# Layer 0's opening: modulation weights summed 512 wide, block 0 half by matmul, and four chunks normalised on GpSimd

## The chip, the cores and the metric

The kernel runs on one core of a Trainium2 chip. The number that counts is the device time of one execution in microseconds (us), on that core. TensorE (PE) does matmuls and transposes, VectorE (DVE), ScalarE (ACT) and GpSimd (POOL) do elementwise work, SyncE (SP) issues the DMAs.

## The reference

Two decoder layers over 512 tokens of 1024 channels, in float32. What the change touches is the beginning of layer 0: the modulation of the normalised input and the first columns of the input projection.

```python
mod = jax.nn.silu(c) @ w_ada + b_ada
shift, scale, gate = jnp.split(mod, 3, axis=-1)
h = rms_norm(x, g_norm) * (1.0 + scale[:, None, :]) + shift[:, None, :]
z = h @ w_in
```

`c` is one vector of 1024 values, `w_ada` has 3 x 1024 columns per layer. Three token mixers (forgetting attention, sparse attention with an indexer, stick-breaking attention), their merge and an output projection follow; none of that is changed.

## The kernel before

Channels lie on the 128 partitions and tokens along the free axis, so `x` is eight chunks (k = 0 to 7) of 128x512. Every float32 matmul is made of three: each operand is split into a high part (`hi`, L117, a copy on ScalarE) and a low part (`lo`, L121, a subtraction, on VectorE), and high x high, low x high and high x low are added in PSUM (`mm3`). The names `wh`/`wl`, `hH`/`hL`, `tm`/`pr` are such pairs, for weights, for the normalised and modulated input, and for two gate columns' weights.

`first_layer` is layer 0's opening, the first 77 us or so. In it the order of VectorE, ScalarE and GpSimd is the program's own, written out by hand (as PE's and SP's are throughout), so an instruction waits for the one written before it on its engine.

- The eight transposed chunks `xc` (`mix`) and the row of 1/rms values are made; `rb` is that row broadcast over the partitions, in PSUM. `norm(k)` multiplies: `xn[k] = xc[k] * rb` (`vs<-mix,pt`, L886).
- The rest goes in four blocks b = 0 to 3, of 256 channels, two chunks each. `load_ada(b)` loads the shift and the scale weights of the block (eight k chunks of 128 input channels, each 128x256 for shift, part 0, and for scale, part 1). `ada_sums(b)` makes silu(c) times weights, summed over the input channels: k = 0 to 3 are scaled in place by ScalarE (L895) and added by GpSimd (L897), k = 4 to 7 are multiplied and added by VectorE (`scalar_tensor_tensor`, L902). The two sums (`fm` for scale, `tmp` for shift) are summed over partitions by matmuls of one column against ones (`pa`), and VectorE adds the biases (`mod`, L911, L914).
- `chunks(b)` does the multiply and add of scale and shift on two chunks (VectorE, L930), then `hi` and `lo` into `hH`, `hL`.
- `unit(u, b)` is a unit of six 512-column matmuls that adds the block's two chunks into the output column u. u = 0 to 3 are single columns (weights `wt`, split for four chunks at a time by `split_single`), u = 4 and 5 the gate columns (weights from `split_gates(b)`, `tm` and `pr`).

PE's order per block is units 0, 1, 4, 5 of block b, then the `pa` matmuls of block b+1, then units 2 and 3 of block b. In block 3 the rope tables (`rope_tables`, L242 to L270) and the small projection's weights follow on VectorE and ScalarE instead of a next block's sums.

## Time and profile before

| what | value |
|---|---|
| median of 3 runs | 1300.32 us (1298.90 to 1304.62) |
| the profiled execution | 1303.22 us |
| its span in the profile | 1301.3 us |
| mean granted clock of PE | 0.983 |
| PE busy | 1237.4 us, 95% of the span |
| VectorE busy | 978.0 us, 75% |
| ScalarE busy | 728.3 us, 56% |
| GpSimd busy | 170.2 us, 13% |

The span runs from the first to the last instruction that the profile shows; the execution is 1.9 us longer. Times below are counted from the span's start. [...]

### The profile page before, as it was taken

Reading aid. Unit: us, or ns where it says so; the run is one execution under the profiler, and the core shown is the slowest. Engines: PE = TensorE matmul, PEld = TensorE weight load, DVE = VectorE, ACT = ScalarE, POOL = GpSimd, SP = SyncE. Lnnn points to the kernel's source line nnn. Section 1 sums busy time; section 2 is a strip of 40 time slices with the busy share of each in tenths; the row PEclk is TensorE's granted clock in tenths of the full one; section 3 lists DMA queues with packets and bytes.
Section 4 is the critical chain, followed back from the end, with each engine's and each line's share of the span. In section 5 each row is a group of like instructions: output and inputs, shape, how many; then the busy total and the mean of one; then the engine's idle time right before and its main releaser. Section 6 shows DMA issues by size and latency. Waiting matters only on the chain.

```text
span 1301.3 us, 19557 instructions
## 1 busy us (share of the span) xinstructions
PE 1237.4 (95%) x6970; PEld 1073.9 (83%) x6970; DVE 978.0 (75%) x2065; ACT 728.3 (56%) x1450; POOL 170.2 (13%) x367
## 2 busy tenths in 40 slices
PE   4799999999899899999999999999999999999997
PEld 4689888888778688888899988897887888888887
DVE  6768887799999768675667877788898975756553
ACT  5367766575445555554335766666544475665343
POOL 3302132222112000000000212222201100000000
PEclk7899999999999999999999999999999999999999
DMA  9543333233322333444442423223223222323331
GB/s 322 150 142 98 98 98 87 78 113 100 111 74 74 98 98 97 113 119 126 143 131 82 115 65 98 71 76 97 69 78 83 80 81 82 97 70 118 90 105 73
DMA packets 192433, 133.33 MB, mean 102 GB/s; under 512 B 9456, under 2 KB 187200, under 8 KB 192336
## 3 DMA queue, kind: packets, MB, share of 16 engines
q1 hardware_dynamic: 188720, 125.72, 33.4%
q10 hardware_dynamic: 3616, 6.37, 1.5%
q8 instruction: 55, 0.90, 0.3%
q14 instruction: 42, 0.34, 0.1%
HBM read 125.74 MB, written 6.29 MB: 101 GB/s over the span
## 4 chain that ended last, share of the span: by engine, by line
PE 63%; DVE 19%; DMA 8%; issue 4%; ACT 4%; POOL 1%; SPq 0%; DVEq 0%; POOLq 0%; ACTq 0%
PE pg L65 49%; PE pt L65 7%; DMA raw<-in_w_in_dram 5%; PE pa L65 4%; DVE wl L121 3%; PE pt L69 3%; DVE fm L595 2%; ACT wh L117 2%; DVE ada L278 2%; DVE m L541 1%; DVE score L542 1%; DVE pr L596 1%; DVE pt L121 1%; DMA y<-in_w_ada_dram 1%; DVE qst L123 1%
## 5 line engine op out<-in xcount | busy, mean ns | idle before, releaser
L65 PE MATMUL pg<-hH,wh 128*128 128x512 f32 (+1 forms) x824 | 330.1, 401 | 2.0 <-ACT hH L117 1.8
L65 PE MATMUL pg<-hH,wl 128*128 128x512 f32 (+1 forms) x824 | 322.5, 391 | 0.8 <-DVE wl L121 0.8
L65 PE MATMUL pg<-hL,wh 128*128 128x512 f32 (+1 forms) x824 | 322.1, 391 | 0.0
L121 DVE TENSOR_TENSOR wl<-raw,wh 128x1024 fp32r<-128x1024 f32 (+1 forms) x174 | 212.4, 1222 | 102.2 <-ACT wh L117 100.5
L117 ACT ACTIVATE wh<-raw 128x1024 fp32r<-128x1024 f32 (+1 forms) x174 | 183.3, 1055 | 152.2 <-PE pg L65 84.4
L65 PEld LDWEIGHTS pg<-hH,wl 128*128 128x128 f32 x824 | 156.8, 190 | 34.8 <-DVE wl L121 1.0
L65 PEld LDWEIGHTS pg<-hH,wh 128*128 128x128 f32 x824 | 157.3, 191 | 26.6 <-ACT hH L117 1.8
L65 PEld LDWEIGHTS pg<-hL,wh 128*128 128x128 f32 x824 | 157.3, 191 | 24.8 <-DVE hL L121 0.4
L65 PE MATMUL pg<-wh,hH 128*128 128x256 f32 x448 | 128.7, 287 | 0.0
L65 PE MATMUL pg<-wh,hL 128*128 128x256 f32 x448 | 126.5, 282 | 0.0
L65 PE MATMUL pg<-wl,hH 128*128 128x256 f32 x448 | 126.4, 282 | 0.0
L117 ACT ACTIVATE pt<-pt 128x512 fp32r<-128x512 f32 x192 | 82.8, 432 | 69.8 <-PE pt L69 66.8
L65 PE MATMUL pg<-y,wh 128*128 128x512 f32 x384 | 120.7, 396 | 0.6 <-DVE kl L121 0.6
L121 DVE TENSOR_TENSOR pt<-pt,pt 128x512 fp32r<-128x512 f32 x192 | 92.7, 483 | 22.7 <-ACT pt L117 20.9
L552 ACT ACTIVATE pr<-pr,nm 128x128 f32<-128x128 f32 (+3 forms) x128 | 71.5, 558 | 63.2 <-DVE nm L551 62.2
L69 PE MATMUL pt<-ident,pr 128*128 128x128 f32 x480 | 85.1, 274 | 2.7 <-DVE pr L596 2.7
L65 PEld LDWEIGHTS pg<-wl,hH 128*128 128x128 f32 x448 | 85.4, 191 | 0.7
L65 PEld LDWEIGHTS pg<-wh,hH 128*128 128x128 f32 x448 | 85.3, 191 | 0.7
L65 PE MATMUL pa<-pt,vs 128*128 128x512 f32 (+3 forms) x256 | 72.8, 356 | 13.2 <-DVE pt L121 8.7
L65 PEld LDWEIGHTS pg<-wh,hL 128*128 128x128 f32 x448 | 85.4, 191 | 0.0
L554 ACT ACTIVATE pr<-pr,den 128x128 f32<-128x128 f32 (+3 forms) x128 | 70.7, 558 | 21.0 <-DVE den L553 20.4
L65 PEld LDWEIGHTS pg<-y,wh 128*128 128x128 f32 x384 | 70.4, 190 | 13.4 <-PE pg L65 0.9
(251 smaller groups left out, 2384.3 us busy)
## 6 DMA issues: line engine op xcount, KB each, us to landing
raw<-in_w_in_dram SPq DMA_DIRECT2D x130, 512.0 KB, 3.8
raw<-in_w_ada_dram SPq DMA_DIRECT2D x36, 512.0 KB, 3.5
raw<-in_w_out_dram SPq DMA_DIRECT2D x16, 512.0 KB, 3.6
y<-in_w_ada_dram SPq DMA_DIRECT2D x16, 256.0 KB, 5.6
raw<-in_w_br_fox_dram SPq DMA_DIRECT2D x8, 512.0 KB, 3.5
raw<-in_w_br_sb_dram SPq DMA_DIRECT2D x8, 512.0 KB, 4.1
yf<-xd ACTq DMA_DIRECT2D x16, 256.0 KB, 2.9
raw<-in_w_br_dsa_dram SPq DMA_DIRECT2D x8, 512.0 KB, 4.8
```

What stands on the lines that cost most here:

```text
L65: self.nc.tensor.matmul(o, s, m, start=first, stop=last, skip_group_check=True)
L69: self.nc.tensor.transpose(o, i, self.ident[:n, :n])
L117: self.nc.scalar.activation(out, in_, AF.Copy, scale=scale)
L121: self.nc.vector.tensor_tensor(out, in_, hi.bitcast(F32), ALU.subtract)
L123: self.nc.vector.scalar_tensor_tensor(out, in_, scale, hi.bitcast(F32), ALU.mult, ALU.subtract)
L278: nc.vector.scalar_tensor_tensor(acc, v[:, j, :], self.sc[:, k:k + 1], acc, ALU.mult, ALU.add)
L541: self.pin(nc.vector.max(m8, s))
L542: nc.vector.match_replace(s, m8, s, SENT)
L552: nc.scalar.activation(p, p, AF.Exp, bias=nm, scale=-1.0, accum_out=den)
L554: nc.scalar.activation(p, p, AF.Copy, scale=den)
L595: nc.vector.tensor_tensor_scan(rev, rev, rev, 1.0, ALU.mult, ALU.bypass)
L596: nc.vector.tensor_tensor(s[:, :n - 1], s[:, :n - 1], u[:, 1:n], ALU.mult)
```

## The change

Six things change, all in `first_layer`:

- `load_ada` loads one 256 KB piece per k chunk, with shift and scale weights side by side (128 x 2 x 256); before, a piece held one part of two or four k chunks. The bytes are the same. There are eight DMAs a block (blocks 1 and 3 had six).
- A sum over k is done for both parts at once, in instructions of 512 columns. In block 0, k = 0 to 3 are not summed by any engine beforehand: PE multiplies them by silu(c) directly, as 16 one-column matmuls. k = 4 to 7 are VectorE's.
- In blocks 1 to 3, `ada_start(b)` has ScalarE scale k = 0 and 1 and GpSimd add them, VectorE does k = 2 to 7. The call of `ada_start` stands behind the gates' split of the block before.
- The multiply and add of `chunks` is an Identity activation of ScalarE with scale and bias, ahead of each `hi`.
- The low part of the gate weights is subtracted by GpSimd. The gates' split now follows the sums and the chunks in the program.
- The norms of chunks 4 to 7 are done by GpSimd, from `rs`, a copy of `rb` to SBUF that ScalarE makes; those of chunks 2 and 3 stand behind VectorE's split of the single columns.

```diff
--- before.py
+++ after.py
@@ -818,23 +818,16 @@
 
         def load_ada(b):
 
-            ada[b] = [[None] * KC, [None] * KC]
-
-            def piece(part, k0, n, tag, bufs):
-                v = self.t([P, n, 256], F32, tag, bufs)
-                src = w_ada[k0 * P:(k0 + n) * P, part * D + b * 256:part * D + b * 256 + 256]
-                nc.sync.dma_start(v, src.rearrange("(k p) n -> p k n", p=P))
-                ada[b][part][k0:k0 + n] = [v[:, i, :] for i in range(n)]
-            if b % 2:
-                for part in (1, 0):
-                    piece(part, 0, 4, "raw", 2)
-            else:
-                for k0 in (0, 2):
-                    for part in (1, 0):
-                        piece(part, k0, 2, "y", 8)
-            for k0 in (4, 6):
-                for part in (1, 0):
-                    piece(part, k0, 2, *(("pt", 4) if b % 2 else ("y", 8)))
+            ada[b] = []
+            for k in range(KC):
+                if b % 2 and k < 4:
+                    if k % 2 == 0:
+                        v = self.t([P, 2, 2, 256], F32, "raw", 2)
+                    ada[b].append(v[:, k % 2])
+                else:
+                    ada[b].append(self.t([P, 2, 256], F32, *(("pt", 4) if b % 2 else ("y", 8))))
+                src = w_ada[k * P:(k + 1) * P, 0:2 * D].rearrange("p (t n) -> p t n", t=2)[:, :, b * 256:b * 256 + 256]
+                nc.sync.dma_start(ada[b][k], src)
 
         load_single(0, 0)
         load_ada(0)
@@ -885,30 +878,31 @@
         def norm(k):
             nc.vector.tensor_tensor(xn[k], xc[k], rb, ALU.mult)
 
+        def ada_start(b):
+            v = ada[b]
+            for k in range(2):
+                nc.scalar.activation(v[k], v[k], AF.Copy, scale=self.sc[:, k:k + 1])
+            nc.gpsimd.tensor_tensor(v[0], v[0], v[1], ALU.add)
+
         def ada_sums(b):
 
             pt = self.ps("a")
-            accs = {}
-            for part in (1, 0):
-                v = ada[b][part]
-                for k in range(4):
-                    nc.scalar.activation(v[k], v[k], AF.Copy, scale=self.sc[:, k:k + 1])
-                    if k:
-                        nc.gpsimd.tensor_tensor(v[0], v[0], v[k], ALU.add)
-            for part in (1, 0):
-                v = ada[b][part]
-                acc = accs[part] = self.t([P, 256], F32, "fm" if part else "tmp", 2)
-                for k in range(4, KC):
-                    nc.vector.scalar_tensor_tensor(acc, v[k], self.sc[:, k:k + 1], v[0] if k == 4 else acc,
-                                                   ALU.mult, ALU.add)
-            for part in (1, 0):
-                for c in range(2):
-                    o = 2 - 2 * part + c
-                    self.mm(pt[:, o:o + 1], accs[part][:, c * P:(c + 1) * P], self.ones, o == 0, True)
+            v = ada[b]
+            k0 = 2 if b else 4
+            acc = self.t([P, 2, 256], F32, "fm", 2)
+            for k in range(k0, KC):
+                if b == 0 and k == k0:
+                    nc.vector.tensor_scalar(acc, v[k], self.sc[:, k:k + 1], None, ALU.mult)
+                else:
+                    nc.vector.scalar_tensor_tensor(acc, v[k], self.sc[:, k:k + 1], acc if k > k0 else v[0], ALU.mult, ALU.add)
+            ops = ([] if b else [(v[k], self.sc[:, k:k + 1]) for k in range(4)]) + [(acc, self.ones)]
+            for n, (x, y) in enumerate(ops):
+                for o in range(4):
+                    self.mm(pt[:, o:o + 1], x[:, o // 2, (o % 2) * P:(o % 2 + 1) * P], y, n + o == 0, n + 1 == len(ops))
             c = slice(2 * b, 2 * b + 2)
             for part in (1, 0):
                 base = 24 + 8 * part + 2 * b
-                nc.vector.tensor_tensor(mod[part][:, c], pt[:, 2 - 2 * part:4 - 2 * part], self.prm[:, base:base + 2], ALU.add)
+                nc.vector.tensor_tensor(mod[part][:, c], pt[:, 2 * part:2 * part + 2], self.prm[:, base:base + 2], ALU.add)
                 if part:
                     g = 8 + 2 * b
                     nc.vector.scalar_tensor_tensor(mod[1][:, c], mod[1][:, c], 1.0, self.prm[:, g:g + 2], ALU.add, ALU.mult)
@@ -923,11 +917,11 @@
         def split_gates(b):
             gw[b] = [self.t([P, 2, 256], F32R, "tm", 2), self.t([P, 2, 256], F32R, "pr3", 2)]
             self.hi(gw[b][0], raws["g", b])
-            self.lo(gw[b][1], raws["g", b], gw[b][0])
+            nc.gpsimd.tensor_tensor(gw[b][1], raws["g", b], gw[b][0].bitcast(F32), ALU.subtract)
 
         def chunks(b):
             for k in (2 * b, 2 * b + 1):
-                nc.vector.tensor_scalar(xn[k], xn[k], mod[1][:, k:k + 1], mod[0][:, k:k + 1], ALU.mult, ALU.add)
+                nc.scalar.activation(xn[k], xn[k], AF.Identity, scale=mod[1][:, k:k + 1], bias=mod[0][:, k:k + 1])
                 self.hi(self.hH[:, k, :], xn[k])
             for k in (2 * b, 2 * b + 1):
                 self.lo(self.hL[:, k, :], xn[k], self.hH[:, k, :])
@@ -945,17 +939,22 @@
                     w = [x[:, k - 2 * b, (u - 4) * P:(u - 3) * P] for x in gw[b]]
                 self.mm3(ps, *w, h[0][k], h[1][k], k == 0, k == KC - 1)
 
-        for k in range(4):
-            norm(k)
+        rs = self.t([P, S], F32, "tmp", 2)
+        nc.scalar.copy(rs, rb)
+        for k in range(4, KC):
+            nc.gpsimd.tensor_tensor(xn[k], xc[k], rs, ALU.mult)
+        norm(0)
+        norm(1)
         split_single(0, 0)
         ada_sums(0)
         chunks(0)
         split_single(1, 0)
         split_gates(0)
+        ada_start(1)
         split_single(2, 0)
         split_single(3, 0)
-        for k in range(4, KC):
-            norm(k)
+        norm(2)
+        norm(3)
         for b in range(4):
             if b < 2:
                 load_ada(b + 2)
@@ -971,12 +970,14 @@
             for u in (0, 1, 4, 5):
                 unit(u, b)
             if b < 3:
-                split_gates(b + 1)
+                ada_sums(b + 1)
+                chunks(b + 1)
                 if b == 1:
                     split_single(0, 2)
                     split_single(1, 2)
-                ada_sums(b + 1)
-                chunks(b + 1)
+                split_gates(b + 1)
+                if b < 2:
+                    ada_start(b + 2)
                 if b == 1:
                     split_single(2, 2)
                     split_single(3, 2)
```

VectorE's rows around block 0's sums, from the first norm on. `y` are the pieces of the weights, `fm` and `tmp` the sums. Before:

```order
L886 TENSOR_TENSOR vs_228<-mix_153,pt_221 128x512
L886 TENSOR_TENSOR vs_228<-mix_154,pt_221 128x512
L886 TENSOR_TENSOR vs_228<-mix_155,pt_221 128x512
L886 TENSOR_TENSOR vs_228<-mix_156,pt_221 128x512
L121 TENSOR_TENSOR wl_95<-qst_102,wh_94 128x512
L902 SCALAR_TENSOR_TENSOR fm_254<-y_112,sc_150,y_104 128x256
L902 SCALAR_TENSOR_TENSOR fm_254<-y_112,sc_150,fm_254 128x256
L902 SCALAR_TENSOR_TENSOR fm_254<-y_116,sc_150,fm_254 128x256 x2
L902 SCALAR_TENSOR_TENSOR tmp_259<-y_114,sc_150,y_106 128x256
L902 SCALAR_TENSOR_TENSOR tmp_259<-y_114,sc_150,tmp_259 128x256
L902 SCALAR_TENSOR_TENSOR tmp_259<-y_118,sc_150,tmp_259 128x256 x2
```

After:

```order
L879 TENSOR_TENSOR vs_230<-mix_155,pt_223 128x512
L879 TENSOR_TENSOR vs_230<-mix_156,pt_223 128x512
L121 TENSOR_TENSOR wl_95<-qst_102,wh_94 128x512
L895 TENSOR_SCALAR fm_246<-y_112,sc_152 128x512
L897 SCALAR_TENSOR_TENSOR fm_246<-y_114,sc_152,fm_246 128x512
L897 SCALAR_TENSOR_TENSOR fm_246<-y_116,sc_152,fm_246 128x512
L897 SCALAR_TENSOR_TENSOR fm_246<-y_118,sc_152,fm_246 128x512
L905 TENSOR_TENSOR mod_10_91<-pa_245,prm_148 128x2
L908 SCALAR_TENSOR_TENSOR mod_10_91<-mod_10_91,prm_148 128x2
L905 TENSOR_TENSOR mod_9_90<-pa_245,prm_148 128x2
```

Two norms stand ahead of the split `wl_95` now, where there were four. The eight multiply-adds of 256 columns are one multiply and three multiply-adds of 512.

GpSimd's rows from the power of the row of 1/rms values on, up to the last block's sums. `raw` and `y` are weights to be summed, `pr` the gates' low parts. Before:

```order
L313 TENSOR_TENSOR rstd_143<-rstd_143,mhalf_83 128x4
L897 TENSOR_TENSOR y_104<-y_104 128x256
L897 TENSOR_TENSOR y_104<-y_104,y_108 128x256 x2
L897 TENSOR_TENSOR y_106<-y_106 128x256
L897 TENSOR_TENSOR y_106<-y_106,y_110 128x256 x2
L897 TENSOR_TENSOR raw_128<-raw_128 128x256 x3
L897 TENSOR_TENSOR raw_130<-raw_130 128x256 x3
L897 TENSOR_TENSOR y_291<-y_291 128x256
L897 TENSOR_TENSOR y_291<-y_291,y_295 128x256 x2
```

After:

```order
L313 TENSOR_TENSOR rstd_145<-rstd_145,mhalf_83 128x4
L945 TENSOR_TENSOR vs_231<-mix_159,tmp_235 128x512
L945 TENSOR_TENSOR vs_231<-mix_160,tmp_235 128x512
L945 TENSOR_TENSOR vs_231<-mix_161,tmp_235 128x512
L945 TENSOR_TENSOR vs_231<-mix_162,tmp_235 128x512
L920 TENSOR_TENSOR pr_77_283<-kh_122,tm_282 128x512
L885 TENSOR_TENSOR raw_128<-raw_128 128x512
L920 TENSOR_TENSOR pr_96_369<-yf_142,tm_368 128x512
L885 TENSOR_TENSOR y_295<-y_295,y_297 128x512
L920 TENSOR_TENSOR pr_111_463<-kh_319,tm_462 128x512
L885 TENSOR_TENSOR raw_388<-raw_388 128x512
L920 TENSOR_TENSOR pr_115_531<-yf_402,tm_530 128x512
```

Four norms stand where the sums of block 0 were. The gates' low parts and one add a block follow.

ScalarE's rows in block 3, from the weights that it splits in block 2 to the load of the rope's table (`hH` of block 3 is the last one). Before:

```order
L117 ACTIVATE wh_98<-kl_311 128x512
L117 ACTIVATE wh_100<-yf_313 128x512
L117 ACTIVATE tm_531<-yf_410 128x512
L895 ACTIVATE raw_398<-raw_398,sc_150 128x256 x4
L895 ACTIVATE raw_400<-raw_400,sc_150 128x256 x4
L117 ACTIVATE hH_226<-vs_229 128x512 x2
L269 ACT_TABLE_LOAD
```

After:

```order
L117 ACTIVATE wh_94<-qst_311 128x512
L117 ACTIVATE wh_96<-kh_313 128x512
L117 ACTIVATE tm_462<-kh_319 128x512
L884 ACTIVATE raw_388<-raw_388,sc_152 128x512 x2
L117 ACTIVATE wh_98<-kl_315 128x512
L117 ACTIVATE wh_100<-yf_317 128x512
L924 ACTIVATE vs_231<-vs_231,mod_9_90,mod_10_91 128x512
L117 ACTIVATE hH_228<-vs_231 128x512
L924 ACTIVATE vs_231<-vs_231,mod_9_90,mod_10_91 128x512
L117 ACTIVATE hH_228<-vs_231 128x512
L117 ACTIVATE tm_530<-yf_402 128x512
L269 ACT_TABLE_LOAD
```

The second halves of `wh_94` and `wh_96` stand here now. Eight scales have become two, and each `hH` has an Identity activation ahead of it.

## Rows read from the trace of the kernel before

**Rows 1.** The page of the profile: the busy time of each engine with its share of the span, and the chain that ended last by engine.

```profile
PE 1237.4 (95%) x6970; PEld 1073.9 (83%) x6970; DVE 978.0 (75%) x2065; ACT 728.3 (56%) x1450; POOL 170.2 (13%) x367
...
PE 63%; DVE 19%; DMA 8%; issue 4%; ACT 4%; POOL 1%; SPq 0%; DVEq 0%; POOLq 0%; ACTq 0%
```

**Rows 2.** The view by stretches of time in layer 0's opening. Columns: stretch (us), its length, then PE, PE's weight loads, VectorE, ScalarE and GpSimd busy us (and instructions), granted clock of PE (1.00 is the upper level), DMA share, GB/s.

```profile
15.70:25.00 9.30, 2.05 (x9) 1.88 (x9) 7.05 (x15) 1.63 (x5) 3.45 (x5) 0.50 1.11 335
25.00:29.30 4.30, 4.30 (x10) 3.09 (x11) 4.30 (x8) 4.30 (x10) 0.39 (x1) 0.50 1.10 348
29.30:33.00 3.70, 3.65 (x16) 2.66 (x14) 3.67 (x6) 1.94 (x5) 3.46 (x5) 0.99 1.14 321
...
59.20:63.90 4.70, 1.25 (x9) 1.17 (x9) 3.82 (x7) 0.00 (x0) 3.26 (x36) 0.96 0.64 144
```

**Rows 3.** Timeline of PE. Columns: start, duration of the group, engine, line, operation, output<-inputs, shape, count, and in brackets the idle time ahead and what ended it.

```profile
22.20 1.01 PE L65 MATMUL pa<-ones,tmp 128*128 128x1 f32 x4 [0.95 <-DVE tmp L902]
24.97 0.79 PE L65 MATMUL pg<-hH,wh 128*128 128x512 f32 x1 [1.76 <-ACT hH L117]
...
37.86 0.77 PE L65 MATMUL pg<-hH,wh 128*128 128x512 f32 x1
...
50.34 0.61 PE L65 MATMUL pa<-ones,tmp 128*128 128x1 f32 x4 [1.29 <-DVE tmp L902]
50.80 0.48 PE L65 MATMUL pg<-hH,wh 128*128 128x512 f32 x1
...
63.92 0.78 PE L65 MATMUL pg<-hH,wh 128*128 128x512 f32 x1
...
82.87 0.36 PE L65 MATMUL pt<-wh,hH 128*128 128x208 f32 x1 [1.04 <-ACT mix L993]
```

**Rows 4.** Timeline of VectorE (DVE) around block 0's sums, same columns.

```profile
13.05 2.48 DVE L886 TENSOR_TENSOR vs<-mix,pt 128x512 f32<-128x512 f32 x4 [0.67 <-PE pt L69]
15.45 0.94 DVE L121 TENSOR_TENSOR wl<-qst,wh 128x512 fp32r<-128x512 f32 x1
17.01 0.93 DVE L902 SCALAR_TENSOR_TENSOR fm<-y,sc,y 128x256 f32<-128x256 f32 x1 [0.62 <-POOL y L897]
17.98 2.21 DVE L902 SCALAR_TENSOR_TENSOR fm<-y,sc,fm 128x256 f32<-128x256 f32 x3
20.10 0.48 DVE L902 SCALAR_TENSOR_TENSOR tmp<-y,sc,y 128x256 f32<-128x256 f32 x1
20.62 1.53 DVE L902 SCALAR_TENSOR_TENSOR tmp<-y,sc,tmp 128x256 f32<-128x256 f32 x3
23.25 0.16 DVE L911 TENSOR_TENSOR mod<-pa,prm 128x2 f32<-128x2 f32 x1 [1.10 <-PE pa L65]
...
23.71 1.00 DVE L930 TENSOR_SCALAR vs<-vs,mod,mod 128x512 f32<-128x512 f32 x2
```

**Rows 5.** Timeline of GpSimd (POOL) in 15.9 to 16.5, same columns.

```profile
15.93 1.05 POOL L897 TENSOR_TENSOR y<-y,y 128x256 f32<-128x256 f32 x1
```

**Rows 6.** Groups of instructions by form, over the whole program. Columns: line, engine, operation, names, shapes, count, then busy us and mean ns of one, then idle time before and its cause.

```profile
L692 POOL MEMSET kl<- 64x512 f32 x32 | 16.8, 525 | 164.4 <-PE pt L65 163.7
...
L897 POOL TENSOR_TENSOR y<-y,y 128x256 f32<-128x256 f32 x8 | 6.4, 803 | 0.6
...
L897 POOL TENSOR_TENSOR y<-y 128x256 f32<-128x256 f32 x4 | 3.0, 740 | 10.5 <-ACT y L895 10.5
...
L197 POOL MEMSET pen<- 128x128 f32 x1 | 0.2, 205 | 0.0
...
L527 DVE SCALAR_TENSOR_TENSOR score<-tmp,iw,score 128x512 f32<-128x512 f32 x14 | 10.6, 757 | 3.7 <-ACT tmp L521 3.5
...
L886 DVE TENSOR_TENSOR vs<-mix,pt 128x512 f32<-128x512 f32 x8 | 5.0, 680 | 0.7 <-PE pt L69 0.7
...
L121 DVE TENSOR_TENSOR wl<-kl,wh 128x512 fp32r<-128x512 f32 x2 | 1.4, 683 | 0.0
...
L751 ACT ACTIVATE tm<-mix 128x512 f32<-128x512 f32 x6 | 3.8, 634 | 0.0
...
L754 ACT ACTIVATE mix<-mix,prm 128x512 f32<-128x512 f32 x4 | 2.9, 725 | 0.1
```

**Rows 7.** Timelines of VectorE in the later blocks, same columns as rows 3.

```profile
31.76 0.96 DVE L902 SCALAR_TENSOR_TENSOR fm<-pt,sc,raw 128x256 f32<-128x256 f32 x1
...
35.40 1.53 DVE L902 SCALAR_TENSOR_TENSOR tmp<-pt,sc,tmp 128x256 f32<-128x256 f32 x3
...
48.75 1.53 DVE L902 SCALAR_TENSOR_TENSOR tmp<-y,sc,tmp 128x256 f32<-128x256 f32 x3
...
58.05 0.94 DVE L902 SCALAR_TENSOR_TENSOR fm<-pt,sc,raw 128x256 f32<-128x256 f32 x1 [2.27 <-POOL raw L897]
...
61.67 1.53 DVE L902 SCALAR_TENSOR_TENSOR tmp<-pt,sc,tmp 128x256 f32<-128x256 f32 x3
...
67.02 0.16 DVE L242 CAST pf<-pi 128x4 f32<-128x4 int32 x1
```

**Rows 8.** Timeline of ScalarE (ACT): block 0's `hH`, and the end of the opening.

```profile
13.32 3.30 ACT L895 ACTIVATE y<-y,sc 128x256 f32<-128x256 f32 x8
24.29 1.15 ACT L117 ACTIVATE hH<-vs 128x512 fp32r<-128x512 f32 x2 [7.67 <-DVE vs L930]
...
82.22 1.57 ACT L993 ACTIVATE mix<-pt 128x512 f32<-128x512 f32 x3
```


## The prediction, made before the changed kernel was run

> **What bounds the kernel now.** The page comes first: PE is busy for 95% of the span and heads the chain that ended last, so time can only be won or lost where PE stands still [rows 1]. The change touches layer 0's opening alone, the first 77 us or so; behind it the order on every engine is the same. The view by stretches shows what the opening costs: stretches in which PE is busy for a quarter of the time or less while VectorE works, and a lower granted clock in and behind the first of them [rows 2]. The rows of PE give the gaps: the first 512-column matmul starts at 24.97, and later ones, after a wait, at 37.86, 50.80 and 63.92 [rows 3]. In each gap PE waits for VectorE's column sums of block b, then runs one-column matmuls `pa`, then goes on. So per block four things are on the path: the end of the sums, the `pa` rows behind it, the modulation of two chunks, and (block 3) the rope tables that VectorE makes next. From the rope's first row (67.02) a fixed chain runs to ScalarE's last `mix` at 82.22 and PE's restart at 82.87 [rows 3, 7, 8]. That chain is what passes a shift on: 15.85 us from rope start to restart. After 83 us PE is the bound, and I let a shift pass through unchanged.
>
> The second thing to see is how VectorE and GpSimd slow each other. The same 128x256 multiply-add takes 0.93 and 0.83 us at 17.01 and 17.98, while GpSimd adds, and 0.48 to 0.51 at 20.10 and later, when GpSimd is done; the split `wl` at 15.45 takes 0.94, and lone ones 0.68 [rows 4, 5, 6]. GpSimd's add at 15.93 takes 1.05 against 0.80 on average [rows 5, 6]. I read this as taking turns: one VectorE instruction with two SBUF inputs per GpSimd instruction, the VectorE one ending with or after it. The norms `vs<-mix,pt` read one input from PSUM and take 0.68 on average, as ever, beside GpSimd [rows 6]. The change puts 128x512 work with two SBUF inputs on GpSimd just where VectorE makes block 0's sums.
>
> **The prices not in the trace.** GpSimd's `tensor_tensor` of 128x512: the 128x256 one takes 0.80, and memsets of 128 and 512 columns take 0.205 and 0.525, so some 0.1 does not grow with size. 0.1 + 2 x 0.63 = 1.36 if alone with its inputs. Low bound 0.74 (no growth, the faster of the two 256-wide groups), high bound 1.6 (all doubled) [rows 6]. I take 1.36, as the fixed part is seen in the nearest rows, plus 0.14 for a change of turn (the 15.93 row lost 0.25 to one).
> [...]
> VectorE's 128x512 multiply-add alone is 0.757, a multiply 0.49 to 0.54. ScalarE's 128x512 copy is 0.53 in a row (two in 1.15), 0.634 as one instruction without a pointer and 0.725 with one: 0.09 a pointer, so Identity with scale and bias is 0.81, bounds 0.63 and 0.9 [rows 6, 8].
>
> **Block 0.** Now: sums end at 20.62 + 1.53 = 22.15, four `pa` rows from 22.20 last 1.01, modulation from 23.25, two multiply-adds at 23.71, `hH` at 24.29, PE at 24.97 [rows 3, 4, 8].
> After: ScalarE first copies `rb` (0.58 as other copies, 13.05 to 13.65), then GpSimd normalises four chunks: 4 x 1.5 = 6.0, to 19.7. VectorE has two norms fewer (2 x 0.62 = 1.24), `wl` to 15.4, then one multiply and three multiply-adds. Alone they end at 15.4 + 0.54 + 3 x 0.75 = 18.2. One per GpSimd turn, they end at 16.9, 18.4, 19.9, and the last, alone, at 20.9: 1.2 earlier than 22.15.
> PE's 16 direct matmuls are 32 rows. Four rows last 0.61 at the upper level and 1.01 at the lower [rows 3], pitch 0.11 to 0.22: 3.5 to 6.9 us from 13.1, done by 16.6 to 20.0 and hidden under the sums; if these end at 18 they are not. Their y tiles have landed by 15, since ScalarE and VectorE use y tiles from 13.3 and 17.0 now [rows 4, 8].
> Behind the sum, all eight `pa` rows must run where four did: +0.86 at the lower level. Identity for the multiply: +0.25 before the first `hH`. Sum: -1.2 + 0.86 + 0.25 = -0.1, PE at 24.9. The second chunk comes 1.35 behind the first (now 0.53), about what three matmuls take there.
>
> **Blocks 1 and 2.** Each later sum is six 512-wide multiply-adds, 6 x 0.757 = 4.6, where eight 256-wide ones take 5.2 (31.76 to 36.93, four of them beside GpSimd's adds) [rows 7]. Their start: VectorE has fewer norms and no gate `lo`, but `wl_99` waits for ScalarE, which does two scales (2 x 0.7) ahead of `wh_98`; I get 32.0 against 31.76, end 36.6, minus 0.35, then four more `pa` rows, +0.9: PE at 38.4 against 37.86. Block 2: start 45.0 as now, end 49.6 against 48.75 + 1.53 = 50.28, four more rows at the upper level +0.45: 50.6 against 50.80 [rows 3, 7].
>
> **Block 3** decides. ScalarE now has Identity, `hH`, Identity, `hH` (2.6 us where two `hH` take 1.15), then `wh_94`, `wh_96`, the gate, two scales, `wh_98`, `wh_100`: done about 58.1. VectorE's four `wl` follow it, `wl_99` held by GpSimd's add. The sums start at 59.2 (now 58.05), end at 63.8 (now 63.20): +0.6. PE's unit 0 also waits about a microsecond for `wl_95` at 54, under the longer wait for the sums. Eight `pa` rows instead of four: +0.9 to 1.1. Unit 2 starts at 65.6 against 63.92. Then Identity and `hH` in turn, 2.5 us on ScalarE, replace two multiplies and two overlapped `hH`: another +0.9 to 1.0. Rope starts at 69.6 against 67.02 [rows 3, 7]: +2.6. ScalarE sits idle there today, but nothing else fills the wait either.
> A block's end is not a sum over blocks: PE waits in each, so only what stands at rope's start is left. +2.6, less a tenth for ends that round away: **+2.5 us**. DMA: the bytes are the same; four more issues, two in block 1 and two in block 3, lie on SP's queue far ahead of their use, since the sums wait for GpSimd's adds and not for a DMA (2.27 idle at 58.05, released by GpSimd [rows 7]). I count nothing; without that cover a piece that lands late would hold the six multiply-adds of its block by its lateness.
> This profile is 1303.22 (span 1301.3 and 1.9 around it) beside a median of 1300.32. 1303.22 + 2.5 = 1305.7 on its own scale; on the scale of the median, 1302.8.
> The bounds by GpSimd's price: at 1.6 four norms add 1.0 and block 3's gate and add 0.5: +4.0. At 0.74 and with no turns, block 0's sums end 2.7 earlier (18.2) and `wl` 0.2; the adds that the sums of blocks 1 to 3 wait for save 0.5 each: 2.5 - 2.9 - 1.5 = -1.9, and -4.4 if PE's clock is up as well (2.0 for block 0's rows as in (c), 0.5 for `pa` rows). By Identity's price, 0.18 less or 0.1 more, twice in the last block: under 0.4 either way.
>
> **Rivals.**
> (a) As above: +1 to +4, 55%.
> (b) Turns don't bite: a 512-wide GpSimd op is near 0.8 or leaves VectorE its stream. Sums of block 0 end at 18 to 18.5, PE starts some 3 us earlier, and every later chain starts earlier with it: -1.9 to -4.4 by the bounds above, 1296 to 1298.4. For it: VectorE's last ops at 20.62 run at 0.51, half the slowed price, and the norms from PSUM don't mind GpSimd at all; against it, all rows with two SBUF inputs beside GpSimd are slow [rows 4]. 22%.
> (c) The clock stays up. PE stood for 12 us and its granted clock was 0.50 in 15.7 to 29.3, full in the stretch after [rows 2]. With 32 rows in that gap it may be at full speed when unit 0 comes: ten 512-column rows fill 4.30 us at the lower level, sixteen 3.65 at the upper [rows 2], so 0.43 and 0.23 each, and 2.0 us for ten. But block 1's sums then wait for ScalarE's and VectorE's queues, so about 1.0 gets through: 1301 to 1302, or 1300 with the same in block 3. 10%.
> (d) Slower: the four norms hold VectorE longer, since GpSimd's op is above 2 us. With p for one and its turn, block 0's sum ends at 13.7 + 4p + 1.0: with p = 2.2, 23.5, which is 2.6 later than in (a), and block 3's gate and add put on 2 x 0.7: 2.5 + 2.6 + 1.4 = +6.5, or 1306.8. It decides from p = 2.2. The 256-wide 0.80 speaks against it [rows 6]; 13% with a lower clock that lasts into unit 3 of block 3 (1.6 more).
> [...]
>
> **How the numbers follow.** 0.5% is 6.5 us, about what a measurement of this kernel can tell from no change. (a), (b) and (c) lie within it, all but an edge of (b), where still more of the clock comes back: 8% faster. (d) gives slower, with an edge of (a): 12%. Same: 80%. The predicted time is (a)'s 1302.8. (a)'s own range is 1301 to 1304.5; the whole one takes in (b) and (c) down to 1296 and (d)'s start, 1307.
>
> **What would show it.** Right: GpSimd rows 128x512 of 1.2 to 1.6 from 13.7 to 19.7; VectorE's multiply-adds at 1.3 to 1.5 each beside them and 0.76 in blocks 1 to 3; sum of block 0 done near 20.9 and PE's first 512-column row near 24.9; 32 `pa` rows done before that sum; `pa` eight rows behind it; rope starting at 69 to 70 and PE's restart 2 to 3 us later. Wrong: sums done by 18.5, a rope start at 67 or less, a granted clock of 1.00 in 25 to 29, or a shift at 83 us that the rest of the program doesn't keep.

## The result and the profile after

The changed kernel takes 1309.23 us (median of 9 runs, 1307.54 to 1313.19), the kernel before 1300.34 (9 runs): a ratio of 1.0067 [1.0049, 1.0085], or 8.9 us slower. The forecast was 1302.8 in 1296 to 1307. It is missed, on the slow side.

The profiled execution took 1313.16 us (span 1311.4), 9.9 more than the one before (1303.22), so what follows accounts for some 10 us of one execution. First the page, the busy time and the chain, which answer to [rows 1]:

```profile
PE 1247.3 (95%) x7002; PEld 1082.3 (83%) x7002; DVE 972.1 (74%) x2039; ACT 725.7 (55%) x1433; POOL 166.8 (13%) x354
...
PE 65%; DVE 17%; DMA 6%; issue 5%; ACT 4%; POOL 1%; DVEq 0%; POOLq 0%; ACTq 0%
```

Every engine but PE has less to do, PE has 32 rows more (7002 against 6970). PE's timeline in the opening, which answers to [rows 3]:

```profile
12.78 3.63 PE L65 MATMUL pa<-sc,y 128*128 128x1 f32 x32
21.07 1.86 PE L65 MATMUL pa<-ones,fm 128*128 128x1 f32 x8 [4.66 <-DVE fm L897]
25.02 0.79 PE L65 MATMUL pg<-hH,wh 128*128 128x512 f32 x1 [2.08 <-ACT hH L117]
...
37.13 1.83 PE L65 MATMUL pa<-ones,fm 128*128 128x1 f32 x8 [3.76 <-DVE fm L897]
...
50.32 1.02 PE L65 MATMUL pa<-ones,fm 128*128 128x1 f32 x8 [0.71 <-DVE fm L897]
...
64.98 1.84 PE L65 MATMUL pa<-ones,fm 128*128 128x1 f32 x8 [3.56 <-DVE fm L897]
66.68 0.77 PE L65 MATMUL pg<-hH,wh 128*128 128x512 f32 x1
...
89.24 0.54 PE L65 MATMUL pt<-wh,hH 128*128 128x208 f32 x1 [3.15 <-ACT mix L994]
```

PE's first 512-column row comes at 25.02 (24.97 before), block 3's unit 2 at 66.68 (63.92), and the restart behind the rope at 89.24 (82.87), after a wait of 3.15 where there were 1.04. VectorE's timeline, which answers to [rows 4, 7]:

```profile
13.60 1.29 DVE L879 TENSOR_TENSOR vs<-mix,pt 128x512 f32<-128x512 f32 x2 [1.29 <-ACT tmp L943]
14.80 0.69 DVE L121 TENSOR_TENSOR wl<-qst,wh 128x512 fp32r<-128x512 f32 x1
15.40 1.49 DVE L895 TENSOR_SCALAR fm<-y,sc 128x512 f32<-128x512 f32 x1
16.93 4.09 DVE L897 SCALAR_TENSOR_TENSOR fm<-y,sc,fm 128x512 f32<-128x512 f32 x3
...
60.16 0.74 DVE L897 SCALAR_TENSOR_TENSOR fm<-raw,sc,raw 128x512 f32<-128x512 f32 x1
...
70.80 2.33 DVE L242 CAST pf<-pi 128x4 f32<-128x4 int32 x1
73.23 0.29 DVE L252 TENSOR_TENSOR rq<-pf,fr 128x128 f32<-128x128 f32 x1
```

A cast of four elements takes 2.33 us, 0.16 before [rows 7]. GpSimd's timeline, which answers to [rows 5, 6], shows why:

```profile
13.64 6.04 POOL L945 TENSOR_TENSOR vs<-mix,tmp 128x512 f32<-128x512 f32 x4 [1.40 <-ACT tmp L943]
...
56.39 1.44 POOL L920 TENSOR_TENSOR pr<-kh,tm 128x512 fp32r<-128x512 f32 x1 [10.94 <-ACT tm L117]
57.79 1.29 POOL L885 TENSOR_TENSOR raw<-raw 128x512 f32<-128x512 f32 x1
...
70.75 1.28 POOL L920 TENSOR_TENSOR pr<-yf,tm 128x512 fp32r<-128x512 f32 x1 [11.67 <-ACT tm L117]
71.98 1.12 POOL L247 MEMSET fr<- 128x1 f32 x32
```

Block 3's gate subtraction starts 0.05 before the cast, and behind it on GpSimd's queue stand the 32 memsets of the rope's frequencies, without which `rq<-pf,fr` can't start. The memsets end at 73.10, the cast at 73.13, `rq` starts at 73.23. In the kernel before, nothing of GpSimd stood beside the cast at 67.02: the memsets were done by then, behind block 3's adds (its 36 GpSimd instructions in 59.2 to 63.9, [rows 2]).

Then PE's clock, by the view of stretches (columns as in [rows 2]):

```profile
25.00:29.30 4.30, 4.28 (x9) 2.88 (x10) 2.13 (x4) 4.27 (x8) 1.85 (x2) 0.50 1.10 348
...
60.00:64.90 4.90, 1.42 (x7) 0.84 (x5) 4.66 (x7) 0.00 (x0) 0.00 (x0) 0.94 0.53 120
...
89.20:92.00 2.80, 2.76 (x13) 2.76 (x14) 1.08 (x2) 2.77 (x7) 0.00 (x0) 0.50 0.32 112
92.00:96.00 4.00, 4.00 (x25) 4.00 (x25) 1.03 (x5) 1.59 (x5) 0.00 (x0) 0.62 0.59 149
```

The granted clock is 0.50 behind the restart, the lower level; in the kernel before it was 1.00 there:

```profile
82.80:85.60 2.80, 2.73 (x24) 2.73 (x25) 1.08 (x2) 2.77 (x8) 0.00 (x0) 1.00 0.29 102
```

So where the time came from can be read off one table. For each row of PE, matched with its twin in the trace before by counting from the last, it gives how much later (us) it comes (the lag), at some times of the kernel before:

| kernel | 27 us | 52 | 65 | 77 | 90 | 165 | 215 | 565 | end |
|---|---|---|---|---|---|---|---|---|---|
| changed | 0.1 | 0.4 | 2.8 | 4.3 | 9.1 | 9.2 | 10.3 | 12.0 | 10.4 |
| e1 memsets first | 0.0 | 0.0 | 2.2 | 3.4 | 6.3 | 6.2 | 7.5 | 9.1 | 8.1 |
| e2 norms on VectorE | -2.1 | -0.6 | 1.7 | 3.3 | 5.3 | 5.2 | 8.2 | 11.3 | 12.6 |
| e3 multiply on VectorE | -0.4 | -1.9 | -1.0 | 0.4 | 3.2 | 3.3 | 4.9 | 6.2 | 5.5 |
| e4 gate low on VectorE | -0.1 | 0.1 | 2.3 | 3.1 | 5.7 | 6.0 | 9.2 | 11.1 | 11.3 |
| e5 multiply, gate early | -0.2 | -1.5 | 0.3 | 0.2 | 0.4 | 0.3 | 2.1 | 1.4 | 3.2 |
| e6 sums ahead | -3.6 | -7.0 | -8.3 | -7.5 | -7.7 | -7.8 | -4.6 | -3.3 | -2.8 |
| e7 before, 16 dummies | 0.2 | 0.2 | 0.4 | 1.5 | 0.2 | 0.2 | 1.9 | 3.1 | -1.4 |
| e8 as e6, PE rows as before | -1.0 | -4.4 | -5.4 | -4.9 | -4.9 | -5.1 | -5.1 | -3.3 | -4.6 |
| e9 before, 64 dummies | 16.2 | 16.2 | 15.5 | 16.2 | 16.0 | 16.0 | 16.3 | 16.1 | 14.2 |

Changed against before: 0.4 in block 2, 2.8 at block 3's unit 2, 6.4 at the restart, 2.7 more by the clock, 1.3 more by the end. These are single executions, and one kernel's executions differ by some 6 us: the ends say less than the steps.

### The profile page after: what moved, and what is told of

It reads as the page before. It is cut to its first block, busy times and chain, and to the rows that moved or that the text cites. A ratio compares the mean times of both kernels' runs of the same rounds, so it can differ in the third digit from the quotient of the medians.

```text
span 1311.4 us, 19555 instructions
## 1 busy us (share of the span) xinstructions
PE 1247.3 (95%) x7002; PEld 1082.3 (83%) x7002; DVE 972.1 (74%) x2039; ACT 725.7 (55%) x1433; POOL 166.8 (13%) x354
## 4 chain that ended last, share of the span: by engine, by line
PE 65%; DVE 17%; DMA 6%; issue 5%; ACT 4%; POOL 1%; DVEq 0%; POOLq 0%; ACTq 0%
PE pg L65 50%; PE pt L65 8%; DMA raw<-in_w_in_dram 5%; PE pa L65 4%; DVE wl L121 4%; PE pt L69 3%; ACT wh L117 2%; DVE fm L595 2%; DVE ada L278 2%; DVE pt L121 1%; DVE score L542 1%; DVE m L541 1%; DVE pr L596 1%; DVE fm L897 1%; DVE qst L123 1%
## 5 line engine op out<-in xcount | busy, mean ns | idle before, releaser
L65 PEld LDWEIGHTS pg<-hL,wh 128*128 128x128 f32 x824 | 157.5, 191 | 24.9 <-DVE hL L121 0.9
L65 PE MATMUL pa<-pt,vs 128*128 128x512 f32 (+3 forms) x256 | 73.5, 358 | 14.2 <-DVE pt L121 8.4
```

The lines of the kernel that those rows point to most:

```text
L65: self.nc.tensor.matmul(o, s, m, start=first, stop=last, skip_group_check=True)
```

## The experiments

The theory behind the experiments had three parts: the multiply on ScalarE lengthens the path in each block; GpSimd's moved subtraction holds the rope; something behind 83 us loses more. The rivals were that the norms on GpSimd are what costs, and that GpSimd doesn't hold the cast: only the memsets hold `rq`.

**e1: the 32 memsets ahead of the subtraction** (`rope_freq` holds them, cut out of `rope_tables`)

```diff
+                if b == 2:
+                    self.rope_freq()
                 split_gates(b + 1)
```

> The changed kernel, with GpSimd's 32 memsets of the rope's frequencies issued ahead of the last gate's subtraction instead of behind it. Theory (GpSimd's queue): VectorE's cast at the rope's start takes 0.16 instead of 2.33, the rope's first multiply comes 0.3 after it instead of 2.4, PE's restart comes 2.1 earlier (89.2 to 87.1), its idle time there falls from 3.15 to about 1.1 and the clock does not drop behind it (2.7 more): 1303.5 to 1305.5 in all. [...] Rival (the loss lies elsewhere): 1308 or more.

Measured: 1310.4 us, 1.0066 [1.0042, 1.009]: no change that the times show. The cast on VectorE and the subtraction on GpSimd:

```profile
70.28 1.26 DVE L250 CAST pf<-pi 128x4 f32<-128x4 int32 x1
```

```profile
70.23 1.28 POOL L925 TENSOR_TENSOR pr<-yf,tm 128x512 fp32r<-128x512 f32 x1 [10.47 <-ACT tm L117]
```

With the memsets gone the cast still takes 1.26, and ends with GpSimd's subtraction: GpSimd holds the cast itself, and the memsets held it for another 1.1. The restart comes at 87.52, 1.7 earlier than in the changed kernel, and the lag at 90 us falls by 2.8. PE still waits 2.30 there, and the granted clock behind it is 0.63 for 4.5 us, which loses 1.6 more:

```profile
87.52 0.36 PE L65 MATMUL pt<-wh,hH 128*128 128x208 f32 x1 [2.30 <-ACT mix L1001]
```

```profile
87.50:92.00 4.50, 4.48 (x26) 4.48 (x26) 1.91 (x5) 2.88 (x7) 0.00 (x0) 0.63 0.22 66
```

The median does not follow; its interval is some 3 us either way, so the times can't tell 2.8 us from nothing.

**e2: the norms back on VectorE**

```diff
-        rs = self.t([P, S], F32, "tmp", 2)
-        nc.scalar.copy(rs, rb)
-        for k in range(4, KC):
-            nc.gpsimd.tensor_tensor(xn[k], xc[k], rs, ALU.mult)
-        norm(0)
-        norm(1)
+        for k in range(4):
+            norm(k)
```

(Chunks 4 to 7 then stand where those of 2 and 3 stood.)

> The changed kernel, with all norms back on VectorE where they stood before (four ahead of block 0's sums, four behind the single columns' splits) and without ScalarE's copy of the row. Theory (taking turns): block 0's multiply takes 0.5 and its multiply-adds 0.75 each, so the sums end at 13.05 + 2.5 + 0.6 + 0.5 + 2.3 = 18.9 instead of 21.0 and PE's first 512-column row comes at 22.9 instead of 25.0; block 1's sums start 0.9 earlier, as four norms (2.5) now stand where two did; 1307 to 1308.5 in all. Rival (VectorE's work itself is the bound, GpSimd does not hold it): the two more norms come on top, sums end at 22.2, PE's first row at 26.2, 1310 or more.

Measured: 1313.92 us, 1.0091 [1.0068, 1.0114]. Block 0's sums on VectorE, without GpSimd beside them, and PE's clock behind the restart:

```profile
16.00 0.48 DVE L895 TENSOR_SCALAR fm<-y,sc 128x512 f32<-128x512 f32 x1
16.52 2.33 DVE L897 SCALAR_TENSOR_TENSOR fm<-y,sc,fm 128x512 f32<-128x512 f32 x3
```

```profile
88.00:92.00 4.00, 3.87 (x34) 3.87 (x35) 2.02 (x5) 3.90 (x9) 0.00 (x0) 1.00 0.23 82
```

The multiply falls from 1.49 to 0.48, three multiply-adds from 4.09 to 2.33, and PE's first row comes at 22.85: the two engines do take turns. But of the 2.2 us gained 1.0 is left from block 1 on, and the rope starts at 69.78, 1.0 earlier. So the norms on GpSimd are 1.0 of the 3.78 us at the rope, and not the loss as a whole. Two things stay odd. PE waits 3.05 us before its restart at 88.13, and yet the clock is 1.00 behind it; and the kernel loses 3.0 between 165 and 215 and 4.4 after, so that it ends slower than the changed one. The expected total was missed.

**e3: the chunks' multiply back on VectorE**

```diff
-                nc.scalar.activation(xn[k], xn[k], AF.Identity, scale=mod[1][:, k:k + 1], bias=mod[0][:, k:k + 1])
+                nc.vector.tensor_scalar(xn[k], xn[k], mod[1][:, k:k + 1], mod[0][:, k:k + 1], ALU.mult, ALU.add)
```

> The changed kernel, with the multiply and add of the chunks back on VectorE. Theory (ScalarE's order Identity, high part, Identity, high part is on the path in every block): from the biases to the second high part's end takes 1.6 instead of 2.7, block after block, so the rope starts 3 to 4 us earlier (70.8 to about 67.3) and the whole is 1304.5 to 1306.5. Rival (only the last block's stage is on the path, the others hide under VectorE's queue): rope 1.0 to 1.5 earlier, 1307.5 to 1308.5.

Measured: 1308.24 us, 1.0044 [1.0028, 1.0061]. PE's timeline:

```profile
24.57 0.80 PE L65 MATMUL pg<-hH,wh 128*128 128x512 f32 x1 [1.76 <-ACT hH L117]
...
61.63 1.46 PE L65 MATMUL pa<-ones,fm 128*128 128x1 f32 x8 [3.56 <-DVE fm L897]
```

PE starts 0.45 earlier in block 0, but block 3's sums are done 3.35 earlier than in the changed kernel, and the rope starts at 66.05, before the 67.02 of the kernel before. One Identity ahead of each `hH` is worth 4.75 us at the rope, and ScalarE's queue passes it on from block to block, since the splits `wh` that VectorE's sums stand behind come later each time: the sums start 1.2 earlier than in the changed kernel in block 1 (31.11 for 32.31), 2.25 in block 2, 3.35 in block 3. The cast, still beside GpSimd, takes 2.31; restart at 84.44. The rope is earlier than the theory had it, yet the total is in the rival's range: 1.6 us go by a granted clock of 0.69 in the 4 us behind the restart (PE waits 2.20 there), and 1.6 between 165 and 215.

**e4: the gates' low parts back on VectorE**

```diff
-            nc.gpsimd.tensor_tensor(gw[b][1], raws["g", b], gw[b][0].bitcast(F32), ALU.subtract)
+            self.lo(gw[b][1], raws["g", b], gw[b][0])
```

> The changed kernel, with the gates' low parts back on VectorE, behind the chunks. GpSimd's memsets of the rope's frequencies then follow the add of block 3 and are done by 60. Theory (queue and turns): the split of the third single column falls from 1.43 and 1.54 to 0.7 to 1.3 (the add still runs beside it), the cast takes 0.16, one subtraction of 0.68 stands ahead of the rope; the rope's first multiply comes at 70.5 to 71.5 instead of 73.23, the clock stays up behind the restart: 1303 to 1305.5. Rival (the work on VectorE costs as much as it frees): 1307 or more.

Measured: 1312.3 us, 1.0071 [1.0048, 1.0095]. VectorE:

```profile
70.96 0.16 DVE L242 CAST pf<-pi 128x4 f32<-128x4 int32 x1
```

The cast is at its old 0.16 with GpSimd idle, `rq` starts at 71.23 (73.23), the restart comes at 86.93 (89.24). So the 2.2 us of the cast are GpSimd's. The expected total is missed: the clock was to stay up and is 0.64 in the 4 us behind the restart (1.6 us lost, after a wait of 2.01), and 3.2 us go between 165 and 215.

**e5: the multiply on VectorE, and block 3's gate split ahead of its sums**

```diff
                 if b == 2:
+                    split_gates(b + 1)
                 ada_sums(b + 1)
```

(with the edit of e3; the other blocks' split stays where the change has it)

> The changed kernel, with the multiply and add of the chunks back on VectorE and the last block's gate split ahead of its sums, so that GpSimd's last subtraction and the 32 memsets behind it are done by 63. Theory (the loss is ScalarE's longer stage in every block plus VectorE's cast held by GpSimd at the rope's start): the cast takes 0.16, the rope's first multiply comes at 66.3 to 67.3 (before the change 67.28, changed 73.23), PE's restart at 82 to 83, no lower clock behind it: within 2 us of the kernel before, a ratio of 0.999 to 1.002. Rival (something else in the later program is lost too): 1.004 or more with the same restart time.

Measured: 1305.95 us, 1.0038 [1.0023, 1.0053]. VectorE and GpSimd:

```profile
56.57 1.77 DVE L121 TENSOR_TENSOR wl<-yf,wh 128x512 fp32r<-128x512 f32 x1
58.27 0.74 DVE L897 SCALAR_TENSOR_TENSOR fm<-raw,sc,raw 128x512 f32<-128x512 f32 x1
...
67.31 0.17 DVE L242 CAST pf<-pi 128x4 f32<-128x4 int32 x1
```

```profile
56.10 1.69 POOL L920 TENSOR_TENSOR pr<-yf,tm 128x512 fp32r<-128x512 f32 x1
57.74 1.12 POOL L247 MEMSET fr<- 128x1 f32 x32
```

The subtraction now costs the split `wl` beside it (1.77 for 0.68) but is out of the rope's way. Lag 0.3 to 0.4 from 90 to 165: the opening takes what it took before, and the kernel is still slower by 0.4%, outside the theory's range and near the rival's. What remains is lost behind 190 us, where the code is the same. The first step lies at ScalarE's `wh<-raw`; ScalarE's row before, and in e5:

```profile
186.54 1.06 ACT L117 ACTIVATE wh<-raw 128x1024 fp32r<-128x1024 f32 x1 [0.83 <-DMA raw<-in_w_in_dram]
```

```profile
188.60 1.06 ACT L117 ACTIVATE wh<-raw 128x1024 fp32r<-128x1024 f32 x1 [2.55 <-DMA raw<-in_w_in_dram]
```

It waits for one load, of which 15 of 16 pieces had landed by 186.92 (in the kernel before all 16 by 186.52) and the last one at 188.58. In that stretch a packet of instructions was fetched, as the view of DMA in 185 to 187 of e5 shows (queue, kind: packets, MB, share of 16 engines); before, that stretch had none, and the fetch came at 188.5:

```profile
q8 instruction: 1, 0.02, 2.8%
```

The page counts 55 such packets of 0.90 MB together, 16.4 KB each. I take them for PE's: between two of them PE starts 127 matmuls on average in the traces of before and after (98 to 153), ScalarE 11 to 48 instructions. PE has 7002 matmuls with a weight load each, 14,004 instructions, so a packet holds about 255 of them, an estimate from these counts. The 32 rows more in block 0 are 64 instructions, a quarter of a packet: by that every later fetch comes a quarter of a packet earlier in the program, here some 3.4 us (185.4, where PE lags by 0.3), and falls beside other loads. That the fetch is what holds the piece back is read from this coincidence; e7 to e9 test it.

**e6: a version meant to be faster.** The sums of block b + 1 stand ahead of the wait that they used to end: VectorE sums, then the splits, the norms fill its waits, the memsets stand at the start, the gates' low parts are VectorE's, and ScalarE has the multiply in blocks 1 and 2 only. Block 0 keeps its half by matmul. In the diff `ada_vector` holds the multiply-adds, `ada_sums` the `pa` rows and the biases.

```diff
-                ada_sums(b + 1)
-                chunks(b + 1)
+                ada_vector(b + 1)
...
+                ada_sums(b + 1)
+                chunks(b + 1)
```

> A new order of the opening, from what the runs show. Kept of the change: shift and scale rows side by side, 512-wide sums, block 0 half by matmul. Undone: nothing but the rope's memsets (now at the start) is left on GpSimd; norms and gates' low parts are VectorE's, two norms stand ahead of block 0's sums, and VectorE's waits for the column matmuls are filled with norms and gate splits. New: the sums of block b+1 (ScalarE scales one row block, VectorE adds seven) stand ahead of the wait for block b+1's biases and no longer behind ScalarE's scales and GpSimd's add; the multiply is VectorE's in blocks 0 and 3, ScalarE's in blocks 1 and 2. Theory (each block was one serial chain of all engines, some 13 us for 8 to 10 us of PE work): block 0's sums end at 17.6, PE's first 512-column row at 21.5, the second group of block 0 at 31 to 33 (before 37.86), of block 2 at 51 to 54 (before 63.92), the rope starts at 55 to 58 (before 67.02): 1288 to 1293 where the kernel before has 1300.3, a ratio of 0.991 to 0.994. Rival (the loads set the pace, as DMA is saturated up to 43): the later blocks start no more than 3 us earlier, a ratio of 0.997 to 1.000.

Measured: 1300.43 us, 0.9977 [0.996, 0.9995]: the gain is less than half of the expected one, and the ratio is in the rival's range. But the loads don't hold the opening as the rival had it (in the kernel before, DMA's share was 1.05 to 1.14 and 314 to 348 GB/s from 13 to 43): it is 7.7 us shorter (rope start 59.19), and 3.2 of that are given back between 165 and 215, where e5 loses 1.8.

**e7: the kernel before with 16 dummy matmuls.** They write a column that nobody reads, in PE's wait for block 0's sums: the PE instructions of the change, and nothing else of it.

```diff
+            if b == 0:
+                for _ in range(16):
+                    self.mm(pt[:, 8:9], self.ident, self.ones, True, True)
```

> The kernel before the change, with 16 one-column matmuls of constants added on PE ahead of block 0's column matmuls, where PE stands still; nobody reads what they write, no other instruction changes. It has the 64 PE instructions (32 rows and their weight loads) that the change adds, and nothing else of it. Theory (the code fetch): PE's instructions come in pieces of 16 KB, each fetched by a DMA; 64 instructions more put every later fetch at another place of the program, where it falls on weight loads that land late for it. The opening is as before (first 512-column row within 0.3 of 24.97, restart within 0.3 of 82.9), and PE is later by 1 to 3 us by the end of the program, in steps that begin between 180 and 215, as in the changed kernels (after: +1.1 from 180 to the end, with gate and multiply undone: +2.8): ratio 1.001 to 1.0025. Rival (the later loss comes from the order or the timing of the opening): the whole is as before within 0.5 us, ratio 0.9995 to 1.0005.

Measured: 1306.21 us against 1302.62, 1.002 [1.0007, 1.0034]. PE's first row comes at 25.15 and the lag is 0.2 again from 90 to 190, after up to 1.5 in between: the rows themselves are hidden. Then it steps to 1.9. The row of ScalarE is late as in e5:

```profile
188.37 1.06 ACT L117 ACTIVATE wh<-raw 128x1024 fp32r<-128x1024 f32 x1 [2.43 <-DMA raw<-in_w_in_dram]
```

So PE instructions that cost nothing where they stand cost some 0.2% later. How the steps add up to it this trace does not show: the first is won back by 400 (lag 0.1), a second of 3.6 follows at 558 to 562, and that is gone by 1000. (The profiled execution, 1301.75, is the second lowest of twelve; it ends ahead in spite of the steps, which the median does not.)

**e8: e6 with block 0 summed on VectorE like the others.** PE then has 6970 rows, as before, and gives up 2.7 us of head start.

```diff
-            ops = ([] if b else [(v[k], self.sc[:, k:k + 1]) for k in range(4)]) + [(acc, self.ones)]
+            ops = [(acc, self.ones)]
```

> The order with the sums ahead, with block 0 summed like the other blocks (ScalarE scales one row block, VectorE adds seven), so that PE has as many instructions as before the change. Theory (the code fetch): the opening ends 2 to 3 us later than with the matmuls (VectorE's sums of block 0 end at 20.7 instead of 17.6, rope start at 60 to 62 instead of 59.19 where the kernel before has 67.02), but from there the lead over the kernel before stays within 1 us of what it is at 100 us, as the fetches stand where they stood: a lead of 5 to 7 us, ratio 0.9945 to 0.9965. Rival (the lead is lost later whatever the fetches): it falls by 3 us or more after 180, as it did with the matmuls (7.8 to 2.8): ratio 0.998 or more.

Measured: 1298.63 us, 0.9965 [0.9947, 0.9983], 4.0 below the kernel before on its chip. ScalarE's row for the load that came late in e5 and e7 waits no longer than before:

```profile
181.37 1.06 ACT L118 ACTIVATE wh<-raw 128x1024 fp32r<-128x1024 f32 x1 [0.73 <-DMA raw<-in_w_in_dram]
```

PE's first row comes at 23.98, later than e6's 21.34, and the lead of 5 us passes 215 whole; it is 3.3 at 565 and 4.6 at the end. This kernel beats the one before the change and the changed one; from e6 the intervals don't tell it.

**e9: the kernel before with 64 dummy matmuls**, 256 instructions, one whole packet of code by the count in e5: if the place of the fetches is what counts, the step at 190 to 215 should go.

```diff
+            if b == 0:
+                for _ in range(64):
+                    self.mm(pt[:, 8:9], self.ident, self.ones, True, True)
```

> The kernel before the change, with 64 one-column matmuls of constants in the place of the 16: 256 instructions on PE, one piece of 16 KB. They no longer fit into PE's gap, so the opening ends later by some 5 to 9 us, and I compare only what comes behind it. Theory (where a fetch falls): every later fetch stands at the same place of the program as before the change, one piece further on, so PE's lag behind the kernel before is at 100 us what it is at 400, within 0.7, with no step of 1.5 between 190 and 215. Rival (any instructions added on PE lose time later, or such steps come and go by chance): a step of 1 or more between 180 and 215, as with 16.

Measured: 1318.56 us, 1.0137 [1.0115, 1.016]. The dummies cost more than expected, since they run past the sums, by PE's timeline:

```profile
12.88 24.82 PE L65 MATMUL pa<-ones,ident 128*128 128x1 f32 x128
```

But from there the lag is 16.0 at 90 to 190 and 16.3 at 215: no step. The page counts 56 code fetches where the other kernels have 55. The times can't say more: 17.8 us by the ratio, 15.0 to 20.8 by its interval, against 16.0 of lag.

All ten traces together say more than these three. Between 165 and 215 the lag grows by 1.1 to 3.2 in each of the eight kernels with 64 PE instructions more, and by 0.3 or less with none (e8) or 256 (e9). A second step, at 558 to 562, is 1.3 to 3.6 in the same eight and 0.0 in e8 and e9. It follows a load whose last piece landed 1.3 to 1.9 us behind the others between 525 and 541, with a fetch begun 2.6 to 3.1 us ahead of that, in each of the eight and in no other trace. And of the 52 loads, in all eleven traces from 100 us on, whose last piece landed over 1.2 us behind the other 15, 46 had a fetch begun at most 3 us ahead of the 15th piece; of the other 2507 loads 271 had. So late pieces go with fetches, and these two steps with the fetches' place. That each later step of each kernel is a fetch isn't shown: in e2 and e4 other things were moved as well, and lag is also lost and won elsewhere.

## Why the prediction was wrong

**Right.** The opening as far as block 2, within 0.6 us. GpSimd's 512-wide norm takes 1.51 on average beside VectorE (taken 1.36 + 0.14), and the add of block 2, with VectorE idle, 1.29. (The 1.36 does not come out of the 0.80 that the forecast names, which gives 0.1 + 2 x 0.70 = 1.50; it goes with the faster group's 0.74.) The two engines take turns there (VectorE's multiply 1.49 and three multiply-adds 4.09 beside GpSimd, 0.48 and 2.33 without it in e2), and block 0's sum ends at 21.02 (20.9), PE starts at 25.02 (24.9); the eight `pa` rows add 0.85 at the lower level (0.86); Identity takes 0.81 (0.81). The 32 direct rows are hidden, and no row of the opening up to 84 us is released by a DMA, so the smaller pieces cost nothing there. Rivals (b) and (d) fall by these rows: neither 18.5 for the sums nor 2.2 for the norm was near. (c) falls too: the clock was no higher at unit 0 (0.50 in 25 to 29.3, as before).

Two details under the total were off. The first norm waited 0.55 more for ScalarE's copy of the PSUM row that it reads itself; the split `wl` behind it took 0.69, not the 0.94 of before, so the sums started on time. And the multiply with one SBUF input took a turn (1.49) like those with two: the forecast's sum had given it one, but its reading named two inputs as the condition, under which the cast would run free.

**The step that failed first:** "From the rope's first row (67.02) a fixed chain runs ... 15.85 us from rope start to restart." It is not fixed. The rope starts at 70.80 and the restart comes 18.44 later: 2.2 of the 2.6 more are the cast, held by GpSimd. The working listed what the change puts on VectorE's and ScalarE's queues in block 3 and left out that the last gate's `pr` now stands on GpSimd's queue behind the chunks (before it was VectorE's, ahead of the sums), with 32 memsets behind it that the rope needs (the rows of GpSimd ahead of the prediction stop just short of these). e1, e4 and e5 show both halves of it: the subtraction beside the cast, and the memsets behind the subtraction. Of the other 0.4, 0.3 is one of the rope's rows beside GpSimd's next two memsets (0.52 at 73.82, for 0.23).

**The term that was too small:** the rope's start, +2.6 forecast, +3.78 measured. Block 3's sums began at 60.16, not 59.2: `wl` of block 3 took 1.54 beside GpSimd, and its `wh` stood behind the Identity stages of earlier blocks. e3 shows that the Identity costs 4.75 us at the rope, while the forecast had it at 0.25 in block 0 and 0.9 to 1.0 in block 3 and let blocks 1 and 2 round away ("only what stands at rope's start is left"). They did not: what VectorE waited for there was ScalarE.

**The second step that failed:** "After 83 us PE is the bound, and I let a shift pass through unchanged." PE's longer waits were followed by a lower clock: 0.50 and 0.62 in the 6.8 us behind the wait of 3.15 in the profiled execution, 2.7 us lost, and 0.63, 0.69 and 0.64 in the 4 to 4.5 us behind waits of 2.0 to 2.3 in e1, e3 and e4, 1.6 each (nothing in e5, e6 and e8, whose last wait is 0.8 to 1.2; but nothing in e2 either, with 3.05, so the wait before the restart alone does not decide it; what does stays open). And there are 64 more PE instructions, which move the code fetches (from 188.5 to 185.4 in e5): e7 has these by themselves as 0.2%, about 2.6 us of the 8.9 (0.9 to 4.4 by its interval).

Sum for the profiled execution, whose span is 10.1 longer, against the +2.5 forecast: 1.2 at the rope's start, 2.2 for the cast, 0.4 from there to the restart, 2.7 for the clock, 1.3 later (in the main 1.1 between 165 and 215, 1.5 between 540 and 565, 1.5 won back between 900 and 1000): 7.8, where 7.6 are missing. Whether the clock fell in the other eight executions no trace shows; their mean granted clock is 0.980 to 0.984, and the two above 1313 have 0.980. The median's 8.9 thus may hold less than 2.7 of it.

## What to carry to other kernels

When work is moved to an engine that was idle, write out that engine's whole queue behind it, down to the smallest instruction that someone waits for: a 1.3 us subtraction was cheap, and the cast that it and the 32 memsets behind it held was the bill, 2.2 us. A stage put on the path of every block was paid once per block, where the queue that carries it feeds the next block's start: without the Identity (0.81 each) the sums start 1.2, 2.25 and 3.35 us earlier in blocks 1 to 3, and the rope 4.75 (e3). And the long PE-bound tail did not pass the shift on unchanged: it grew by 2.7 us where the granted clock was 0.50 to 0.62, and 64 instructions added on PE went with a step of 1.1 to 3.2 us between 165 and 215, where a code fetch stood some 3.4 us earlier (e5).

## What the runs showed of the hardware

- In these runs instructions of VectorE with one SBUF input were held by GpSimd too: a 128x512 multiply took 1.49 beside it (0.48 in e2, without it), a cast of 128x4 1.26 to 2.33 (0.16 in e4), while two norms with one input in PSUM took 1.29 beside it, 0.65 each (0.62 in the kernel before). The forecast had not counted on this for the cast.
- Memsets of GpSimd held the cast as well: it ended 0.03 after the last of the 32 in the changed kernel; in e1, where they stood elsewhere, it ended 0.03 after the subtraction. They did not hold a multiply-add with two SBUF inputs: in e5 that at 58.27 took its usual 0.74 with the memsets of 57.74 to 58.86 beside it.
- In e5 and e7 one of a weight load's 16 pieces landed 1.6 to 1.7 us behind the other 15, just after a code fetch of 16 KB, and the engine waited for that last piece. Over all traces such late pieces mostly go with a fetch (46 of 52); that the fetch is the cause is the likeliest reading, and no run turned a fetch alone on or off.
